# Shorter inverse square roots on VectorE, one tile for the query buffers, and nine feature places with a slot for lone weights

## The chip, the core and the metric

The kernel runs on one NeuronCore of a Trainium2 chip. The metric is the device time of one execution in microseconds (us). TensorE (PE) multiplies matrices, VectorE (DVE) and ScalarE (ACT) do elementwise work and move results out of PSUM, GpSimd (POOL) does a little elementwise work, and SyncE (SP) issues DMA transfers. Each engine runs its own instruction list strictly in order; engines wait for each other through semaphores.

## The reference

One block of a network over 2048 tokens of width 1024, with a context of 256 tokens. Both streams are normalised and modulated, projected by one matrix `w_in`, and mixed by 4 gated linear-attention heads (HGRN2) and 4 retention heads, in both directions. Output projection, residual, second norm, a feed-forward part with a convolution of width 3, and a final norm follow.

```python
hx = rmsnorm(x, norm1_g) * (1 + sc1) + sh1            # sc1, sh1 ...: silu(c) @ w_mod + b_mod
hc = rmsnorm(ctx, norm1_g) * (1 + csc1) + csh1
hq, hi, hff, hfb, hg, rq, rk, rv, rg = split(h @ w_in)   # for h = hx and h = hc, 4 heads of 128 each
f = lb + (1 - lb) * sigmoid(hff)                       # and hfb for the backward direction; k = 1 - f
# HGRN2, each direction:   S = diag(f) S + k v^T ;  o = S q      (start state from the context)
hg_o  = rmsnorm((o_f + o_b) * sigmoid(hg), hg_norm_g)
# retention, each direction: R = gamma R + k v^T ;  y = R q      (rope on q and k)
ret_o = rmsnorm(y_f + y_b, ret_norm_g) * silu(rg)
x = x + g1 * (concat(hg_o, ret_o) @ w_out)
gate, up = split((rmsnorm(x, norm2_g) * (1 + sc2) + sh2) @ w_up)
x = x + g2 * ((silu(conv3(gate)) * up) @ w_down)
return rmsnorm(x, final_g)
```

## The kernel before

Every big product is done by `mm3`: both operands are stored as pairs of f16 values (a high part and a remainder), and three matmuls (lines 102 to 104) add high by high, high by low and low by high. On top of that a product of 2 x 2 blocks is done with seven products instead of eight, so each operand exists as seven combined blocks. Seven such blocks of a group of 512 tokens are the **feature blocks**: tiles `hx` for the main stream (512 KB each), `hc` for the context. A combined block is made by a sum on VectorE (lines 455 and 501), a cast to f16 on ScalarE (450) and a subtraction that leaves the remainder on VectorE (451). For each group the tiles of temporary results that `first_blocks` uses are named in a list by `temps`: a string is one tile with both halves side by side, so that cast and subtraction are wide (128x512 in the trace); a pair of names is two narrow tiles and two instructions (128x256).

The 2048 tokens are four groups, 3 down to 0. `heads` runs over 8 heads and 4 groups. Each step weaves, instruction by instruction, the sweep of one group (`hg_sweep1`, `ret_sweep1`: decay products over levels 1 to 64, scores, state updates), the second direction of the head before (`hg_sweep2`) and the projections of the next group (`hg_proj`, `ret_proj`). A projection has the units z (gates), q and vg (values and output gate); the names `pa`, `pb`, `pc`, `pd` are its PSUM results, `ct`, `cb`, `cs`, `ta`, `tb` their copies, `w_z`, `w_q`, `w_vg` the split weights. The first head's projections use feature blocks that are made in the same steps: group 2 ahead of the loop, the context and group 1 in step 0, group 0 in step 1. They are stored to DRAM (`hxd`) and every later head loads them again (`hx<-hxd`, line 557) into a ring of `RING` = 10 places of which a group takes seven.

`norm_rows` makes the norms of a group: squares summed on ScalarE and VectorE (409, 411), `ssq` (413), the inverse root, then a scaling of each tile, half on ScalarE (419) and half on VectorE (421), and `transposed` (428, PE, `tp`). The inverse root of these calls is `rstd`, six instructions on GpSimd (lines 72 to 77). A second form, `rstd_v` (84 to 90, VectorE), is called by `head_out` for every group of every head (four columns) and by the last steps of the FFN (one column); the last of these ends the kernel.

`head_weights` loads the raw weights of the next head in 512 KB tiles: two for z, one (lone) for q, two for vg; the last head has lone v and g. All share the tag `wr` with two buffers. A raw tile is squared for its norm (750), later split into f16 pairs (q: 760; pairs: 703 and 704), and its buffer falls free with the last split.

In `hg_sweep1`, K and Q hold the two directions side by side; at each level they are multiplied by running totals `T` (925 and 930), copied for the scores (`Kl` 895, `Ql` 898), and `sc` (908) and `sf` (918) are the score matmuls. The backward queries are kept in `qf` (956), one tile per group: `qf0` to `qf3`.

The code records work in program order and a scheduler with a model of each engine's time sets each engine's instruction list before the run; the list is fixed then. So a change of tiles or of one helper can move instructions elsewhere.

## Time and profile before

| what | value |
|---|---|
| median of 3 runs | 2556.37 us (2556.28 to 2559.72) |
| the profiled execution | 2557.44 us, span 2555.7 us |
| mean granted TensorE clock | 0.99 of full speed |
| GpSimd busy | 386.9 us, 377 instructions |
| DMA moved | 402.36 MB, 157 GB/s over the span |

The profile is one execution; its span is what the trace covers, and the profiled run's own time is 1.74 us longer. An instruction row gives the start in us from the span's start, the duration, engine, line of the code, operation, output<-inputs with shapes, a count where equal rows are put together, and in brackets the engine's idle time ahead of it with the instruction that ended it. A grouped row gives the count, the sum and the mean in ns of one. A window row gives its ends, its length, and busy times with counts by engine.

### The profile page before, as it was taken

What the parts mean: (1) busy time and instruction counts of PE and PEld (TensorE: products, weight loads), DVE (VectorE), ACT (ScalarE), POOL (GpSimd) and SP (SyncE); (2) the same over time, 40 slices, a digit from 0 to 9 for tenths busy, and PEclk for the clock granted to TensorE, in tenths of its full rate; (3) what the DMA queues carried; (4) which work ended last, traced back from release to release, by engine and by line L of the source; (5) the groups of instructions that cost most, each with busy time, mean ns of one, the idle gap of its engine ahead of it and who ended that gap; (6) DMA issues with size and microseconds to landing.
All of it is one profiled execution on the core that took longest, in us unless ns stands there. A gap on an engine that the chain in (4) does not pass through costs nothing.

```text
span 2555.7 us, 56261 instructions
## 1 busy us (share of the span) xinstructions
PE 2476.7 (97%) x22763; PEld 1644.6 (64%) x22763; DVE 1892.4 (74%) x4309; ACT 1354.8 (53%) x2886; POOL 386.9 (15%) x377
## 2 busy tenths in 40 slices
PE   6899999999999999999999999999999999999998
PEld 4688989898899999985454444444444444444443
DVE  6888787878677877875658888887888887224756
ACT  7786666656545544554556565555665555211221
POOL 1100000000000000001230343434343443000000
PEclk8899999999999999999999999999999999999999
DMA  8415243334466767785320233322333338534562
GB/s 313 169 63 193 90 159 131 115 124 142 162 207 211 265 213 247 254 313 194 106 78 30 85 114 120 108 107 99 110 113 104 108 130 301 205 142 157 216 221 78
DMA packets 144788, 402.36 MB, mean 157 GB/s; under 512 B 16143, under 2 KB 16371, under 8 KB 139920
## 3 DMA queue, kind: packets, MB, share of 16 engines
q1 hardware_dynamic: 134976, 381.81, 42.7%
q10 hardware_dynamic: 9248, 16.79, 2.0%
q8 instruction: 178, 2.92, 0.5%
q14 instruction: 82, 0.67, 0.1%
q0 software_dynamic: 304, 0.17, 0.0%
HBM read 302.77 MB, written 95.94 MB: 156 GB/s over the span
## 4 chain that ended last, share of the span: by engine, by line
PE 66%; DVE 16%; issue 6%; ACT 5%; DMA 5%; POOL 1%; SPq 0%; DVEq 0%; ACTq 0%; POOLq 0%
PE pa L102 7%; PE pa L103 7%; PE pa L104 7%; PE pd L104 5%; PE pd L102 5%; PE pd L103 5%; PE pc L102 3%; PE pc L104 3%; PE pc L103 3%; PE pb L102 2%; PE pb L103 2%; PE pb L104 2%; PE opp L103 2%; PE opp L104 2%; PE opp L102 2%
## 5 line engine op out<-in xcount | busy, mean ns | idle before, releaser
L104 PE MATMUL pa<-feat,w 128*128 128x512 f16 x704 | 266.6, 379 | 1.9 <-DVE w L704 1.9
L102 PE MATMUL pa<-feat,w 128*128 128x512 f16 x704 | 263.6, 379 | 4.6 <-ACT ta L596 4.5
L103 PE MATMUL pa<-feat,w 128*128 128x512 f16 x704 | 266.8, 379 | 0.0
L103 PE MATMUL pd<-wd,actl 128*128 128x512 f16 x616 | 233.3, 379 | 0.0
L104 PE MATMUL pd<-wd,actl 128*128 128x512 f16 x616 | 233.3, 379 | 0.0
L102 PE MATMUL pd<-wd,actl 128*128 128x512 f16 x616 | 232.6, 379 | 0.0
L104 PEld LDWEIGHTS <-w 128*128 128x128 f16 x1232 | 120.5, 98 | 147.5 <-DVE w L704 2.6
L103 PEld LDWEIGHTS <-w 128*128 128x128 f16 x1232 | 120.5, 98 | 144.9 <-issue 5.3
L102 PEld LDWEIGHTS <-w 128*128 128x128 f16 x1232 | 120.4, 98 | 142.1 <-ACT w L703 1.3
L103 PEld LDWEIGHTS <-hx 128*128 128x128 f16 x1824 | 179.4, 98 | 8.3 <-issue 6.4
L102 PEld LDWEIGHTS <-hx 128*128 128x128 f16 x1824 | 179.6, 99 | 1.8 <-ACT hx L447 0.2
L104 PEld LDWEIGHTS <-hx 128*128 128x128 f16 x1824 | 179.0, 98 | 1.4 <-DVE hx L448 0.7
L1507 POOL TENSOR_TENSOR ssq<-ssq 128x1 f32<-128x1 f32 x16 | 7.0, 439 | 1111.4 <-ACT junk L1502 1111.4
L1752 ACT ACTIVATE st<-act,modT 128x512 f16<-128x512 f32 x154 | 107.3, 717 | 114.8 <-DVE act L1742 64.9
L102 PE MATMUL pa<-w_vg,hx 128*128 128x128 f16 x896 | 160.6, 220 | 3.0 <-ACT ct L596 1.4
L104 PE MATMUL pa<-w_vg,hx 128*128 128x128 f16 x896 | 160.4, 220 | 0.5 <-DVE hx L448 0.5
L1753 DVE SCALAR_TENSOR_TENSOR st<-act,modT,st 128x512 f16<-128x512 f32 x154 | 142.6, 961 | 24.5 <-ACT st L1752 23.9
L103 PE MATMUL pa<-w_vg,hx 128*128 128x128 f16 x896 | 160.7, 220 | 0.0
L102 PE MATMUL pa<-hx,w_z 128*128 128x256 f16 x512 | 140.9, 275 | 6.4 <-ACT ct L596 4.1
L104 PE MATMUL pa<-hx,w_z 128*128 128x256 f16 x512 | 140.8, 275 | 1.9 <-issue 1.9
L103 PE MATMUL pa<-hx,w_z 128*128 128x256 f16 x512 | 140.9, 275 | 0.5 <-DVE hx L451 0.4
L102 PE MATMUL pc<-feat,w 128*128 128x512 f16 x352 | 133.4, 379 | 0.8 <-ACT w L703 0.8
(545 smaller groups left out, 7219.0 us busy)
## 6 DMA issues: line engine op xcount, KB each, us to landing
hx<-hxd SPq DMA_DIRECT2D x212, 512.0 KB, 5.0
actd<-st SPq DMA_DIRECT2D x154, 256.0 KB, 2.0
actl<-actd SPq DMA_DIRECT2D x28, 1024.0 KB, 5.2
wur<-in_w_up_dram SPq DMA_DIRECT2D x44, 512.0 KB, 3.6
raw<-in_w_in_dram SPq DMA_DIRECT2D x36, 512.0 KB, 4.7
wm<-in_w_mod_dram SPq DMA_DIRECT2D x64, 256.0 KB, 4.2
hxd<-hx SPq DMA_DIRECT2D x28, 512.0 KB, 3.6
wdb<-in_w_down_dram SPq DMA_DIRECT2D x44, 256.0 KB, 4.1
```

The lines of the kernel that those rows point to most:

```text
L102: mm(ps, lhs(0), rhs(0), start=start, stop=False, skip_group_check=True)
L103: mm(ps, lhs(0), rhs(1), start=False, stop=False, skip_group_check=True)
L104: mm(ps, lhs(1), rhs(0), start=False, stop=stop, skip_group_check=True)
L1507: nc.gpsimd.tensor_tensor(ssq[:, 0:1], ssq[:, 0:1], ssq[:, 1:2], ALU.add)
L1752: nc.scalar.activation(p[:, 0], v, AF.Copy, scale=s)
L1753: nc.vector.scalar_tensor_tensor(p[:, 1], v, s, p[:, 0], ALU.mult, ALU.subtract)
```

## The change

1. `rstd_v` has 9 instructions instead of 12: the shift goes, the first guess is made in one integer multiply and add, and one polynomial with four constants takes the place of three Newton steps. It is called 48 times.
2. `norm_rows` calls `rstd_v` for the context and for groups 2, 1 and 0; only group 3 keeps the GpSimd root.
3. Q of a group is one 128 x 1024 product instead of two of 128 x 512 (16 times).
4. The four query tiles are one tile `qfs`. A pair of neighbours can then be one place for temporary blocks: in group 1 seven pairs of narrow casts and subtractions become seven wide ones.
5. `RING` goes from 10 to 9. The place is used for a new tag `wx`, one buffer, for the lone raw weights (q of heads 1 to 3, v of the last head). The shared `wr` is then for pairs (and the lone g).

VectorE has 4166 instructions instead of 4301, ScalarE 2581 instead of 2588, GpSimd 358 instead of 382. SyncE issues the same transfers in another order, and TensorE has the same instructions.

```diff
-RING = 10
+RING = 9
+RSQ = 0.7235660666409525, -0.6910196001212606, 0.7162674493934401, -0.8287177420385489
...
         ts(v, ssq, 1.0 / count, EPS, ALU.mult, ALU.add)
-        ts(t.bitcast(I32), v.bitcast(I32), 1, None, ALU.logical_shift_right)
-        ts(y.bitcast(I32), t.bitcast(I32), -1, 0x5F3759DF, ALU.mult, ALU.add)
-        for _ in range(3):
-            stt(t, y, -0.5, y, ALU.mult, ALU.mult)
-            tt(t, t, v, ALU.mult)
-            stt(y, t, 1.5, y, ALU.add, ALU.mult)
+        ts(y.bitcast(I32), v.bitcast(I32), -0.5, float(0x5F3759DF), ALU.mult, ALU.add)
+        tt(t, y, y, ALU.mult)
+        tt(t, t, v, ALU.mult)
+        ts(v, t, RSQ[0], -RSQ[0], ALU.mult, ALU.add)
+        stt(t, v, RSQ[3], v, ALU.add, ALU.mult)
+        stt(t, t, RSQ[2], v, ALU.add, ALU.mult)
+        stt(t, t, RSQ[1], v, ALU.add, ALU.mult)
+        stt(y, t, 1.0, y, ALU.add, ALU.mult)
...
+        self.qfs = mp.tile([P, NG, G], F32, name="qfs")
...
-        r = self.rstd(self.mp, ssq[:, :nt], nt, D)
+        r = self.rstd(self.mp, ssq[:, :nt], nt, D) if g == NG - 1 else self.rstd_v(ssq[:, :nt], nt, D)
...
-            def load(cols=cols, raws=raws, tags=own.get(nm, ("wr", "wr"))):
+            def load(cols=cols, raws=raws, tags=own.get(nm, ("wx",) if nm in "qv" else ("wr",) * len(cols))):
...
-        for d in range(2):
-            nc.vector.tensor_tensor(Q[:, d], qs, FG[:, 1 - d], ALU.mult)
+        nc.vector.tensor_tensor(Q, view(qs, 0, [[0, 2], [1, G]]), view(FG, G, [[-G, 2], [1, G]]), ALU.mult)
...
-                self.mp.tile([P, G], F32, tag=f"qf{slot}", bufs=1, name="qf"))
+                self.qfs[:, slot])
...
-                blocks = self.first_blocks(1, rows(1, zq), self.temps(("ou1", "ou2", ("qf1", "qf2"), "ou3")), "tu")
+                blocks = self.first_blocks(1, rows(1, zq), self.temps(("ou1", "ou2", self.qfs[:, 1:3], "ou3")), "tu")
...
-                blocks = self.first_blocks(0, rows(0, zq), self.temps(("ou2", "ou3", ("qf2", "qf3"), ("gate", "gate"))), "tu")
+                blocks = self.first_blocks(0, rows(0, zq), self.temps(("ou2", "ou3", self.qfs[:, 2:4], ("gate", "gate"))), "tu")
```

In the rows below the changed kernel's line numbers are a few higher than the old one's (925 is 930, 930 is 935, 750 is 756).

First VectorE in step 1, where group 0 is normalised while the sweep of group 2 runs (`x` are the rows to be scaled, `T_...` the running totals). Before:

```order
L413 TENSOR_TENSOR ssq<-sq_2158 128x4
L791 TENSOR_TENSOR T_1930<-T_1891 128x32
L630 TENSOR_TENSOR ct<-pc,ct 128x256
L925 TENSOR_TENSOR K<-K,T_1891 128x2x16x16
L421 TENSOR_SCALAR x_2142<-x_2142,rs_y 128x512
L421 TENSOR_SCALAR x_2144<-x_2144,rs_y 128x512
L421 TENSOR_SCALAR x_2146<-x_2146,rs_y 128x512
L421 TENSOR_SCALAR x_2148<-x_2148,rs_y 128x512
L930 TENSOR_TENSOR Q<-Q,T_1891 128x2x16x16
```

The changed kernel at the same place, from the third instruction of the root's chain:

```order
L87 TENSOR_TENSOR rs_t<-rs_y 128x4
L88 TENSOR_TENSOR rs_t<-rs_t,rs_v 128x4
L89 TENSOR_SCALAR rs_v<-rs_t 128x4
L930 TENSOR_TENSOR K<-K,T_1922 128x2x8x32
L935 TENSOR_TENSOR Q<-Q,T_1922 128x2x8x32
L90 SCALAR_TENSOR_TENSOR rs_t<-rs_v 128x4
L636 TENSOR_TENSOR ct<-pc,ct 128x256
L797 TENSOR_TENSOR T_2252<-FG 128x512
L91 SCALAR_TENSOR_TENSOR rs_t<-rs_t,rs_v 128x4
L930 TENSOR_TENSOR K<-K,T_2252 128x2x128x2
L92 SCALAR_TENSOR_TENSOR rs_t<-rs_t,rs_v 128x4
L93 SCALAR_TENSOR_TENSOR rs_y<-rs_t,rs_y 128x4
```

The scaling of x stood ahead of the 16x16 and 8x32 levels of Q; now both levels of Q stand ahead of the end of the root, and the scaling behind it.

Next SyncE while head 1 is swept and the weights of head 2 are loaded. The raw rows of both kernels read alike; before, the first of these three is head 2's lone q and the next two are its vg:

```order
L557 DMA hx<-hxd_128 128x2048
L557 DMA hx<-hxd_127 128x2048
L742 DMA raw<-in_w_in_dram 128x1024
L557 DMA hx<-hxd_146 128x2048
L557 DMA hx<-hxd_147 128x2048
L742 DMA raw<-in_w_in_dram 128x1024
L557 DMA hx<-hxd_151 128x2048
L742 DMA raw<-in_w_in_dram 128x1024
```

In the changed kernel the lone q of head 2 is the first of the three that stand together, some twenty transfers earlier, with the pair for z behind it:

```order
L748 DMA raw<-in_w_in_dram 128x1024
L563 DMA hx<-hxd_148 128x2048
L563 DMA hx<-hxd_139 128x2048
L563 DMA hx<-hxd_140 128x2048
L748 DMA raw<-in_w_in_dram 128x1024 x3
L563 DMA hx<-hxd_144 128x2048
```

The load of q no longer stands behind the reloads of the group; it is issued when head 1's split of q has run.

Last ScalarE one head on, around the split of head 2's q. Before:

```order
L760 ACTIVATE w_q<-raw,p2s 128x512 x2
L972 COPY ou<-op 128x512
L782 ACTIVATE FG<-pa,dq 128x256
L937 COPY A<-sf 64x4x64 x2
L679 ACTIVATE cs<-pa,dq 128x256
L895 COPY Kl<-K 128x512
L693 ACTIVATE qs<-pa,dq 128x256
L750 ACTIVATE w_vg,ssqw<-raw 128x1024
```

The changed kernel:

```order
L766 ACTIVATE w_q<-raw,p2s 128x512 x2
L788 ACTIVATE FG<-ct,dq 128x256
L977 COPY ou<-op 128x512
L788 ACTIVATE FG<-pa,dq 128x256
L942 COPY A<-sf 64x4x64 x2
L685 ACTIVATE cs<-pa,dq 128x256
L756 ACTIVATE w_q,ssqw<-raw 128x1024
L900 COPY Kl<-K 128x512
L699 ACTIVATE qs<-pa,dq 128x256
```

The square of head 3's q now stands behind the copy to cs, six rows after the split that frees its slot, and ahead of a copy of Kl.

## The prediction

> **What bounds the kernel now.** I read the busy times first, then the stages, then the places inside a stage where TensorE stands still, since TensorE has almost no slack elsewhere.

> ```profile
> PE 2476.7 (97%) x22763; PEld 1644.6 (64%) x22763; DVE 1892.4 (74%) x4309; ACT 1354.8 (53%) x2886; POOL 386.9 (15%) x377
> 0.00:60.00 60.00, 40.16 (x284) 25.63 (x285) 40.71 (x118) 44.85 (x80) 7.99 (x21) 0.83 0.87 333
> 60.00:205.00 145.00, 128.59 (x1940) 112.73 (x1938) 127.06 (x313) 119.53 (x283) 11.92 (x24) 0.93 0.34 127
> 205.00:705.00 500.00, 486.37 (x8408) 449.44 (x8405) 390.44 (x1065) 316.75 (x777) 0.00 (x0) 0.99 0.41 136
> 705.00:1205.00 500.00, 489.90 (x5578) 440.02 (x5579) 384.57 (x1048) 247.83 (x620) 7.57 (x28) 1.00 0.69 238
> 1205.00:2540.00 1335.00, 1325.37 (x6532) 614.10 (x6531) 940.56 (x1737) 624.40 (x1126) 359.42 (x304) 1.00 0.37 132
> 106.70:110.10 3.40, 3.40 (x18) 2.33 (x17) 0.23 (x2) 3.25 (x8) 0.00 (x0) 0.50 0.00 0
> 154.50:161.20 6.70, 6.35 (x97) 6.00 (x98) 5.81 (x13) 5.06 (x12) 0.00 (x0) 0.50 0.02 4
> 332.00:335.30 3.30, 3.30 (x18) 2.35 (x16) 1.25 (x5) 1.62 (x4) 0.00 (x0) 0.50 0.61 243
> ```

> After the page's line on engines come windows: length, then busy time of TensorE, its weight loads, VectorE, ScalarE, GpSimd, then the granted clock, DMA share and GB/s. TensorE is busy for 97% of the span, so only its gaps and the stretches at a lower clock can be won. Its idle time is 19.8 us up to 60, 16.4 from 60 to 205 (feature blocks and norms), 13.6 and 10.1 in the two sweep stages and 9.6 in the 1335 us of the output and the FFN. The last three rows are stretches at clock 0.50: what runs in them takes twice as long, so each costs half its length: 1.7, 3.35 and 1.7 us. The change touches the stages from 60 to 1205 and the very end. The profiled run took 2557.44 us (span 2555.7), 1.07 above the median of 2556.37; the sum is made against 2557.44 and taken over to the median.

> **The end of the kernel.** The last root is alone on VectorE, and the store hangs on it.

> ```profile
> 2548.85 0.15 DVE L84 TENSOR_SCALAR rs_v<-cw 128x1 f32<-128x1 f32 x1
> 2550.97 0.16 DVE L90 SCALAR_TENSOR_TENSOR rs_y<-rs_t,rs_y 128x1 f32<-128x1 f32 x1
> 2551.16 1.42 DVE L1915 SCALAR_TENSOR_TENSOR c<-c,rs_y,fgb 128x512 f32<-128x512 f32 x2
> ```

> These are the first and last of 12 dependent instructions, and the scaling that follows: 2.31 us from 2548.85 to 2551.16, or 0.1925 each. Three fewer: **-0.58 us**, on the path, nothing beside it.

> **The norms of the groups.** Four roots go from GpSimd (6 instructions each) to VectorE (9 each). First group 2 and the context, then group 1, then group 0.

> ```profile
> 64.92 0.16 DVE L413 TENSOR_TENSOR ssq<-sq 128x4 f32<-128x4 f32 x1
> 65.00 0.69 DVE L411 SCALAR_TENSOR_TENSOR junk<-gate 128x512 f16<-128x512 f32 x1
> 68.25 1.68 DVE L421 TENSOR_SCALAR x<-x,rs_y 128x512 f32<-128x512 f32 x4 [1.21 <-POOL rs_y L77]
> 75.00:100.00 25.00, 16.62 (x168) 11.47 (x166) 24.51 (x52) 23.96 (x59) 1.00 (x1) 0.80 0.61 230
> ```

> A bracket is the idle time ahead of the instruction and what ended it. A small instruction with independent work behind it occupies VectorE for 0.08 us (64.92 to 65.00), a dependent one for 0.19. From 75 to 100 VectorE is busy for 24.51 of 25 us, so what two roots add there or just ahead counts in full: 18 instructions, at 0.08 to 0.1925, are 1.4 to 3.5 us; taken at 0.10, near the interleaved price since context work is at hand, 1.8. The idle 1.21 goes. Net **+0.6** (from -1.2, if the additions fall in other gaps, to +3.5, if the idle time comes back).

> ```profile
> 99.00 3.12 POOL L72 TENSOR_SCALAR rs_v<-ssq 128x4 f32<-128x4 f32 x1 [28.55 <-DVE ssq L413]
> 104.12 0.20 POOL L77 TENSOR_TENSOR rs_y<-rs_y,rs_t 128x4 f32<-128x4 f32 x1
> 104.35 1.67 DVE L421 TENSOR_SCALAR x<-x,rs_y 128x512 f32<-128x512 f32 x4 [2.30 <-POOL rs_y L77]
> 104.99 0.58 PE L428 MATMUL tp<-ident,x 128*128 128x128 f32 x3 [1.95 <-DVE x L421]
> 144.95 0.19 POOL L72 TENSOR_SCALAR rs_v<-ssq 128x4 f32<-128x4 f32 x1 [40.63 <-DVE ssq L413]
> 147.95 1.68 DVE L421 TENSOR_SCALAR x<-x,rs_y 128x512 f32<-128x512 f32 x4 [2.02 <-POOL rs_y L77]
> 152.50 0.68 DVE L930 TENSOR_TENSOR Q<-Q,T 128x512 f32<-128x512 f32 x1
> 153.33 0.69 PE L918 MATMUL sf<-Q,K 128*64 128x64 f32 x16 [2.20 <-DVE Q L930]
> ```

> In group 1 the GpSimd chain lasts 5.32 us (99.00 to 104.32); nine instructions on VectorE take 1.73 alone, but 3.2 us of other VectorE work stand in the same stretch. The scaling can start at 102.9 to 103.8 instead of 104.35, so of TensorE's 1.95 us some 0.6 to 1.5 go; I take 1.0. The half-clock stretch that begins at 106.7 is worth 1.7; I take 0.5 of it, since much of the gap remains. **-1.5** (0 to -3.65).

> In group 0 VectorE idles 2.02 us for the root and then scales four tiles (1.68) before the levels of Q on which TensorE waits 2.20 us. Now that Q stands ahead of the scaling and independent levels lie between the root's instructions (nine at 0.10, 0.9 us), Q comes up to 2.02 + 1.68 - 0.9 = 2.8 us earlier, more than the gap: -2.2, and of the 3.35 of the half-clock stretch behind it 0.8. **-3.0** (0 to -5.55). What is late next are the scaled tiles: their transposes have about the cover they had.

> **Wide blocks, one Q.**

> ```profile
> L451 DVE TENSOR_TENSOR hx<-ftmp,hx 128x512 f16<-128x512 f32 x28 | 18.8, 684 | 1.0 <-ACT hx L450 0.9
> L451 DVE TENSOR_TENSOR hx<-ftmp,hx 128x256 f16<-128x256 f32 x28 | 11.0, 417 | 0.9 <-ACT hx L450 0.9
> L872 DVE TENSOR_TENSOR Q<-qs,FG 128x512 f32<-128x512 f32 x32 | 20.7, 684 | 3.4 <-ACT qs L693 3.4
> ```

> Fourteen half-width subtractions become seven wide ones: 7 x (2 x 417 - 684) = 1.05 us of VectorE, and as many casts go from ScalarE. Both have idle time behind 105 us: **-0.3** (0 to -1.0). Sixteen Q products lose one instruction start each, at 0.08 that is 1.3 us of VectorE, beside TensorE's sweeps; it is counted with the next term.

> **Roots in the sweeps.**

> ```profile
> L84 DVE TENSOR_SCALAR rs_v<-ossq 128x4 f32<-128x4 f32 x32 | 5.3, 166 | 20.7 <-ACT qf L996 20.6
> ```

> 32 calls lose 3 instructions: 7.7 us of VectorE at 0.08, 18.5 at 0.1925. VectorE idles for 109 and 115 us in these two stages while TensorE idles for 23.7, so TensorE's own work covers most of it; if that cover were gone, all 18.5 would count. **-2** (0 to -5), nearer to nothing because the chain itself waits 20.6 us for ScalarE. The 16 one-column roots of the FFN lie beside full TensorE: 0, but for the last.

> **The lone query weights.**

> ```profile
> 224.47 1.33 ACT L760 ACTIVATE w_q<-raw,p2s 128x512 f16<-128x512 f32 x2
> 254.69 1.06 ACT L750 ACTIVATE w_z<-raw 128x1024 f16<-128x1024 f32 x1 [4.25 <-DMA raw<-in_w_in_dram]
> 324.45 0.33 SPq L742 DMA_DIRECT2D raw<-in_w_in_dram  x1
> 330.17 1.06 ACT L750 ACTIVATE w_q<-raw 128x1024 f16<-128x1024 f32 x1 [2.62 <-DMA raw<-in_w_in_dram]
> 327.89 0.22 PE L102 MATMUL pa<-w_vg,hx 128*128 128x128 f16 x1 [0.33 <-DVE cb L630]
> 331.63 0.27 PE L102 MATMUL pa<-hx,w_z 128*128 128x256 f16 x1 [2.24 <-ACT ct L596]
> 347.95 1.32 ACT L760 ACTIVATE w_q<-raw,p2s 128x512 f16<-128x512 f32 x2
> 350.90 0.47 ACT L679 ACTIVATE cs<-pa,dq 128x256 f32<-128x256 f32 x1
> 352.53 0.86 ACT L895 COPY Kl<-K 128x512 f32<-128x512 f32 x1 [1.15 <-DVE K L870]
> 479.39 0.22 PE L102 MATMUL pa<-w_vg,hx 128*128 128x128 f16 x1 [0.32 <-DVE cb L630]
> 481.69 0.27 PE L102 MATMUL pa<-hx,w_z 128*128 128x256 f16 x1 [0.80 <-ACT ct L596]
> ```

> Head 2's query weights are asked for at 324.45, when a shared slot falls free, and ScalarE stands for them until 330.17 with the eviction behind it that TensorE needs. With their own slot they are asked for behind head 1's split (224.47) and squared soon after, and the row is gone from this place. Counted: 2.24, the half clock from 332 (1.7), the same gap of 0.80 at head 3, and 0.33 and 0.32 in the small gaps ahead of these: **-5.4** (-2.5, if another raw weight takes the place, to -6.5). But the new slot is freed by the split of the head before, and the next square now stands six rows behind that split. At head 3 the split ends at 349.3, the row ahead of the square (the copy to cs) at 351.4, and a load of this kind took 5.7 us above (324.45 to 330.17): a new ScalarE wait of 2 to 3.6 us, with the copy of Kl behind it that had 1.15 us of slack. **+1.0** (0 to +2.5). Head 2's square stands eight rows behind that split, in a stretch where ScalarE waited 4.25 us for another raw (254.69) and no gap of TensorE followed: 0.

> **Nine places instead of ten.**

> ```profile
> hx<-hxd SPq DMA_DIRECT2D x212, 512.0 KB, 5.0
> ```

> The page's row on reloads of feature blocks: 212 of them, 5.0 us to land. They lie in the 1000 us of the two sweep stages, one per 4.7 us. Seven places belong to the group in work, so three loads ran ahead and now two: by this estimate 9.4 us of cover against 5.0. Where loads bunch, some come late: **+1** (0 to +4).

> **Sum:** -0.6 + 0.6 - 1.5 - 3.0 - 0.3 - 2.0 - 5.4 + 1.0 + 1.0 = -10.2 us: 2547.2 as a profiled run, **2546.2 us** as a median.

> [...] The granted clock stood at 0.50 from 332, right behind a gap of 2.24 us. [...]

> **The rivals.**
> *The gaps close and the half-clock stretches stay.* The sum counted 1.7 + 0.5 + 0.8 = 3.0 for the clock: 2549.2. For it: these gaps are short. Against it: all three stretches start within 2 us of one.
> *The waits only move.* Raw weights still arrive one behind the other and VectorE is full from 75 to 100. If the norms bring nothing (+4.5 against the sum) and head 3's new wait is 2.5 and stalls TensorE as the old one did (+1.5 and the clock, 1.7), the sum is -2.5: 2553.9, within 0.2% (5.1 us, about what a measurement of this kernel can tell from no change).
> *More.* If all the clock comes back (+3.75) and the sweeps give their 5, it is 2546.2 - 6.75 = 2539.5.
> *Slower: the ring of nine.* A group's first reload now waits for one more release. Once loads in a bunch land later than 9.4 us, each of some 30 groups (212 / 7) stalls TensorE. To end above 2561.5 this must cost 15.3 us, 0.5 per group; with 0.6 it is 18, and the time 2563. For it: loads already stand behind each other in one queue. Against it: 5.0 us to land.

> **How the numbers follow.** The sum as it stands 0.40 (own range 2542 to 2551), half clock stays 0.15, more 0.15, waits move 0.21, slower 0.09. The first three are faster: 0.70; same 0.21; slower 0.09. The range 2539 to 2556 takes in all but the slower case and the far end of "more".

> **What will show it.** The last root with 9 instructions, 1.73 us. No POOL wait ahead of the scalings of groups 1 and 0; TensorE's gap of 2.20 on Q gone. No raw load ahead of w_q near 330, no gap of 2 us there, clock 1.0 from 332 to 335; a new ScalarE wait of 2 to 3.6 us on a raw near 351. TensorE's idle time from 60 to 205 below 13 us. Reload waits no larger than before. I am wrong if the half clock stays without a gap, if reloads stall the first projection of a group, or if VectorE's work ahead of 100 us delays the context features by more than the norms save.

## The result, and the profile after

The changed kernel takes 0.9929 of the time before (95% interval 0.9918 to 0.9939), some 18 us less; in a second session 0.9923 (0.9911 to 0.9935). The median is 2540.28 us (6 runs, 2536.66 to 2542.58). The kernel before, run beside it, had 2559.27 (6 runs, 2556.28 to 2561.57). The forecast was 2546.2, range 2539 to 2556: the direction held and the median lies in the range, but the gain is 18 us and not 10. The forecast set out from 2556.37; the ratio on that time gives 2538.2, just under the range, so it is in part luck of the session that the range held.

The page's line on engines of the changed kernel, whose profiled run took 2539.82 us (span 2538.0), and then windows as before:

```profile
PE 2470.5 (97%) x22763; PEld 1640.2 (65%) x22763; DVE 1877.6 (74%) x4174; ACT 1354.5 (53%) x2879; POOL 375.9 (15%) x353
```

```profile
60.00:205.00 145.00, 129.90 (x2051) 115.22 (x2048) 136.25 (x346) 123.78 (x283) 0.00 (x0) 0.96 0.36 133
205.00:705.00 500.00, 493.01 (x8474) 457.31 (x8472) 386.88 (x1031) 319.21 (x788) 0.00 (x0) 1.00 0.41 134
705.00:1205.00 500.00, 492.46 (x5479) 435.02 (x5477) 378.12 (x977) 251.43 (x621) 11.78 (x42) 1.00 0.71 245
325.00:335.00 10.00, 10.00 (x176) 9.07 (x175) 7.13 (x27) 7.16 (x19) 0.00 (x0) 1.00 0.22 84
90.50:100.70 10.20, 5.85 (x38) 4.51 (x37) 10.20 (x28) 8.58 (x27) 0.00 (x0) 0.50 0.51 206
384.00:387.40 3.40, 3.40 (x64) 3.20 (x64) 2.32 (x10) 2.29 (x9) 0.00 (x0) 0.50 0.34 104
```

TensorE does the same instructions. Its idle time in the first sweep stage fell from 13.6 to 7.0 us and in the second from 10.1 to 7.5; from 60 to 205 us it fell only from 16.4 to 15.1. The clock is 1.00 from 325 to 335. Between 60 and 1250 us three stretches at half clock are left: 10.24 us from 90.46, and 3.41 us each from 384.00 and 1025.71. Summed over the trace from 60 to 1250 us, the gaps between TensorE's instructions were 40.1 us and are 29.6, and the time lost to half clock (half of each such stretch: in the one from 331.95 before, the 128x256 matmuls start 0.21 us apart, from 336.37 on 0.11) was 13.7 us and is 8.5. These 15.6 us, 0.6 at the end and 1.4 ahead of 50 us are 17.6 of the 17.7 by which the spans differ.

Where the time came from, by instructions that occur equally often in both kernels (start in the changed kernel less start before, the median over all instructions of a stretch of 25 us; the column on the left is the time before):

| at | difference | since the row above |
|---|---|---|
| 50 | -1.4 | -1.4 |
| 75 to 100 | -0.5 | +0.9: context features |
| 275 to 325 | -7.5 | -7.0: norms of groups 1 and 0, blocks |
| 325 to 350 | -11.7 | -4.1: the gap at 330 |
| 425 to 475 | -10.1 | +1.6 |
| 550 to 575 | -10.6 | -0.6 |
| 600 to 625 | -12.5 | -1.9 |
| 700 to 725 | -16.4 | -3.9: the stall at 671 |
| 1200 | -18.2 | -1.9 |
| 2150 to 2500 | -17.1 | +1.1 |
| end | -17.7 | -0.6 |

At the end the root now lasts from 2531.77 to 2533.50, 1.73 us:

```profile
2531.77 0.15 DVE L85 TENSOR_SCALAR rs_v<-cw 128x1 f32<-128x1 f32 x1
2533.50 1.41 DVE L1920 SCALAR_TENSOR_TENSOR c<-c,rs_y,fgb 128x512 f32<-128x512 f32 x2
```

The gap at 330 is gone; the new wait of ScalarE that the prediction named is there, one head on, and the third row is a gap of TensorE further on that was not foreseen, with the half clock from 384.00 behind it:

```profile
340.80 1.06 ACT L756 ACTIVATE w_q<-raw 128x1024 f16<-128x1024 f32 x1 [1.84 <-DMA raw<-in_w_in_dram]
343.44 0.72 ACT L900 COPY Kl<-K 128x512 f32<-128x512 f32 x1 [0.39 <-DVE K L930]
383.19 0.22 PE L105 MATMUL pc<-w_vg,hx 128*128 128x128 f16 x1 [1.98 <-ACT qs L699]
```

### The profile page after: what moved, and what is told of

It reads as the page before. It is cut to its first block, busy times and chain, and to the rows that moved or that the text cites. A ratio compares the mean times of both kernels' runs of the same rounds, so it can differ in the third digit from the quotient of the medians.

```text
span 2538.0 us, 56102 instructions
## 1 busy us (share of the span) xinstructions
PE 2470.5 (97%) x22763; PEld 1640.2 (65%) x22763; DVE 1877.6 (74%) x4174; ACT 1354.5 (53%) x2879; POOL 375.9 (15%) x353
## 4 chain that ended last, share of the span: by engine, by line
PE 71%; DVE 13%; DMA 6%; ACT 6%; issue 3%; POOL 1%; SPq 0%; DVEq 0%; ACTq 0%; POOLq 0%
PE pa L105 8%; PE pa L106 8%; PE pa L107 8%; PE pd L107 5%; PE pd L106 5%; PE pd L105 5%; PE pc L105 4%; PE pc L106 4%; PE pc L107 4%; PE pb L105 2%; PE pb L106 2%; PE pb L107 2%; PE opp L105 2%; PE opp L106 2%; PE opp L107 2%
## 5 line engine op out<-in xcount | busy, mean ns | idle before, releaser
L106 PEld LDWEIGHTS <-hx 128*128 128x128 f16 x1824 | 179.3, 98 | 10.2 <-issue 8.4
## 6 DMA issues: line engine op xcount, KB each, us to landing
hx<-hxd SPq DMA_DIRECT2D x212, 512.0 KB, 4.9
wur<-in_w_up_dram SPq DMA_DIRECT2D x44, 512.0 KB, 3.6
raw<-in_w_in_dram SPq DMA_DIRECT2D x36, 512.0 KB, 5.3
hxd<-hx SPq DMA_DIRECT2D x28, 512.0 KB, 3.2
```

What stands on the lines that cost most here:

```text
L106: mm(ps, lhs(0), rhs(1), start=False, stop=False, skip_group_check=True)
```

## The experiments

Ratios are to the kernel before in the same session, with 95% intervals. Four runs do one part alone, three undo one part of the changed kernel, the rest test a place.

**The short root alone.** The kernel before with the new `rstd_v` (the first hunk of the change).

> The kernel before with the root of 9 instructions in all 48 calls and nothing else of the change. Theory 1 (the shorter chain itself frees ScalarE and TensorE in the sweeps): the stall of 2.2 us on KTt near 671 and the half clock behind it go (-3.6), 2 to 4 us come from other places of the sweeps, 0.58 at the end: 6 to 8 us faster than before. Theory 2 (the sweeps gained because the whole instruction order changed, not because of the chain): only the 0.58 at the end and at most 1.5 elsewhere, 0.6 to 2 us faster. In both the gap of 2.24 us at 330 and the norms' waits stay as before.

0.9971 (0.9959 to 0.9983), 7.4 us faster, the size that theory 1 had. One place is the stall near 671. Before, TensorE waited there for a copy that stood in ScalarE's list behind the square of the next head's z:

```profile
670.83 1.06 ACT L750 ACTIVATE w_z<-raw 128x1024 f16<-128x1024 f32 x1 [3.49 <-DMA raw<-in_w_in_dram]
672.35 0.59 ACT L948 COPY KTt<-kp 128x512 f32<-128x512 f32 x1
672.99 1.83 PE L952 MATMUL uf<-V,KTt 128*128 128x128 f32 x8 [2.23 <-ACT KTt L948]
```

The raw weights come late because their slot is freed by the last splits of w_vg on VectorE; the load is issued at 666.25, right behind the split of 665.47. These splits stand among the 12 steps of a root. The rows are the first step, that split, the last step, the scaling that uses the root, and TensorE's transposes of its result (`otp`) and of K (`kp`), which is the last work ahead of the stall:

```profile
659.98 0.17 DVE L84 TENSOR_SCALAR rs_v<-ossq 128x4 f32<-128x4 f32 x1 [0.46 <-ACT qf L996]
665.47 0.75 DVE L704 SCALAR_TENSOR_TENSOR w_vg<-raw,p2s,w_vg 128x512 f16<-128x512 f32 x1
667.79 0.16 DVE L90 SCALAR_TENSOR_TENSOR rs_y<-rs_t,rs_y 128x4 f32<-128x4 f32 x1
667.99 0.69 DVE L1018 TENSOR_TENSOR ou<-ou,rs_y 128x512 f32<-128x512 f32 x1
669.28 0.60 PE L1003 MATMUL otp<-ident,ou 128*128 128x128 f32 x4
669.72 1.04 PE L947 MATMUL kp<-ident,K 128*128 128x128 f32 x8
```

The root with the splits between its steps takes 8 us. In the changed kernel it takes 5.2, the load is issued at 653.45, ScalarE waits 1.51 us and TensorE 0.29:

```profile
652.67 0.75 DVE L710 SCALAR_TENSOR_TENSOR w_vg<-raw,p2s,w_vg 128x512 f16<-128x512 f32 x1
653.34 0.68 DVE L1023 TENSOR_TENSOR ou<-ou,rs_y 128x512 f32<-128x512 f32 x1
655.28 0.60 PE L1008 MATMUL otp<-ident,ou 128*128 128x128 f32 x4
655.72 1.04 PE L952 MATMUL kp<-ident,K 128*128 128x128 f32 x8
658.07 1.06 ACT L756 ACTIVATE w_z<-raw 128x1024 f16<-128x1024 f32 x1 [1.51 <-DMA raw<-in_w_in_dram]
659.75 1.16 PE L957 MATMUL uf<-V,KTt 128*128 128x128 f32 x8 [0.29 <-ACT KTt L953]
```

The shorter root did not bring the weights sooner. Counted from an earlier split of w_vg (ends at 659.51 and 646.71) the load is issued 6.74 us later in both kernels, ScalarE's square starts 4.58 and 4.62 us behind the load, and TensorE has started 10074 and 10073 matmuls when it is issued. What moved is the work behind the root. The scaling starts 1.74 us behind the load before, and 0.11 us ahead of it now; so `otp` and `kp` stand earlier in TensorE's list, and 33 matmuls of the projections stand between `kp` and the wait where there were none. TensorE falls idle 6.00 us behind the load instead of 4.51. On ScalarE the copy of `otp` now stands ahead of the square and takes up part of its wait.

With the short root alone the stall is gone too, in the same way. By common instructions 2.6 us of its gain lie here, and some 6 us between 900 and 1200, where TensorE's gaps of 1.0 to 1.8 us at 1014, 1042, 1070 and 1126 are gone or 0.8 at most. A new wait of 2.06 us on KTt at 548 and the half clock behind a gap of 2.13 at 478 take some 5 back.

**The long root in the changed kernel.**

> The changed kernel with the old root of 12 instructions in all calls (sweeps, norms and the end). Theory 1 (chain length matters in the sweeps): 6 to 8 us slower than the changed kernel, with a stall near 660 again. Theory 2 (order, not chain): 1 to 3 us slower, of which 0.58 at the end and up to 1 in the norms.

0.9950 (0.9937 to 0.9962), some 5 us slower than the changed kernel, between the two theories. The stall of TensorE on KTt is back, at 656, with 2.11 us, and no half clock behind it. In all 14 profiles it goes with the root: 1.55 to 2.93 us in the six kernels with 12 instructions, 0.41 or less in the eight profiles with 9. The order goes with it: TensorE falls idle 4.51 us behind the load in all of the six, and runs on until 5.84 to 6.10 us behind it in the eight. That much is shown; that the scheduler sets the transposes earlier because the root's result is ready earlier in its model is argued. In the norms the length made no difference: up to 200 us the two kernels keep step within 0.9 us.

**The slot alone.** The kernel before, with

```diff
-RING = 10
+RING = 9
...
+            def load(cols=cols, raws=raws, tags=own.get(nm, ("wx",) if nm in "qv" else ("wr",) * len(cols))):
```

> The kernel before with nine feature places and the own slot for lone raw weights, nothing else. Theory 1 (the gap at 330 and its half clock go, the new wait of ScalarE one head on costs TensorE little): 4 us gained at 330, 0 to 2 given back from 350 to 425, about 1 gained at 480: 3 to 5 us faster. Theory 2 (nine places cost what the slot gains, since reloads come later): within 1 us of before, with larger waits for hx. The half clock at 332 is a test of its own: if it stays at 0.50 without a gap ahead of it, the gap was not its cause.

0.9967 (0.9955 to 0.9980), 8.4 us faster, more than either theory. The gap at 330 is gone with its half clock (-4.1 by common instructions), as theory 1 said, but 3.4 us came between 100 and 200 us, where no lone weight is loaded: TensorE's wait of 2.20 us on Q was gone, with the norms on GpSimd. The next run was made for that.

**Nine places alone.** `RING = 9` and nothing else.

> The kernel before with nine feature places instead of ten and nothing else: lone weights still share. It does no work less, but the order of the instructions moves. If a place less costs cover, it is 1 to 4 us slower than before, with new waits on hx. If the slot's run gained from 100 to 205 (3.4 us there, where the slot has no load) by the new order that nine places bring, this run is 2 to 4 us faster than before and the wait of 2.20 us at 151 is gone, while the gap of 2.2 us near 330 stays.

0.9980 (0.9969 to 0.9991), 5 us faster, by a change that only takes a buffer away. The scheduler made another order. The wait of 2.20 us on Q at 151 is gone, and the same stretch shows how. VectorE before (prediction) waited 2.02 us for the root; here more work stands in front of it, a second eviction among it, GpSimd's root takes 2.4 us instead of 3.0, and the wait is 0.66:

```profile
146.00 0.42 DVE L630 TENSOR_TENSOR ct<-pc,ct 128x256 f32<-128x256 f32 x1
147.08 1.67 DVE L421 TENSOR_SCALAR x<-x,rs_y 128x512 f32<-128x512 f32 x4 [0.66 <-POOL rs_y L77]
149.27 0.68 DVE L930 TENSOR_TENSOR Q<-Q,T 128x512 f32<-128x512 f32 x1
```

The gap near 330 stays, shorter (1.54 us) and without the half clock, and the one near 478 has grown from 0.80 to 2.56. By the ratios about 3 of the 8.4 us belong to the slot and 5 to the order that came with nine places; but each ratio is known to some 3 us either way, so this split is an estimate. ScalarE's waits for reloads of hx are 3.2 and 3.7 us (at 979 and 1121), where the kernel before has 2.5, 2.3 and 3.2 (734, 983, 1126) and the changed kernel one of 1.1 (1013).

**The shared slots back in the changed kernel** (ten places, no `wx`).

> The changed kernel with ten feature places and all raw weights in the two shared slots. Theory 1 (the slot's gain is the gap at 330): the gap of about 2 us and the half clock come back there, 3 to 5 us slower than the changed kernel. Theory 2 (nine places cost as much as the slot gains): the same time within 1 us.

0.9935 (0.9922 to 0.9947), 1.5 us slower than the changed kernel by the ratios, within their intervals. By common instructions it is 3.0 to 4.3 us behind from 600 to 1100 us; a gap of 1.47 us on the raw weights stands at 323 and one of 1.25 at 471, without half clock behind them. A gap of 2.00 us on KTt at 539, where no lone weight is loaded, costs as much. In exchange the gap of 1.98 us at 381 is gone.

**The norms alone, with the long root.**

```diff
-        r = self.rstd(self.mp, ssq[:, :nt], nt, D)
+        r = self.rstd(self.mp, ssq[:, :nt], nt, D) if g == NG - 1 else self.rstd_v(ssq[:, :nt], nt, D)
```

> The kernel before with the norms of the context and of groups 2, 1 and 0 on VectorE, with the old root of 12 instructions, nothing else. Theory 1 (the norms' own waits are what the stage from 100 to 205 gained): the stage from 100 to 205 is 4 to 7 us shorter, the waits of 1.95 and 2.20 us and the half clock behind them go, and the stage before 100 is up to 2 us longer: 3 to 6 us faster. Theory 2 (that stage gained through the new order, since the run with the slot alone lost the wait of 2.20 us too): 0 to 3 us faster, and a wait of about 2 us stands elsewhere in the stage.

0.9981 (0.9971 to 0.9990), 4.9 us. By common instructions some 7 us were gained from 60 to 205, with both waits gone (theory 1), and some 5.5 given back behind a gap of 1.96 us on Kl at 214 and one of 2.30 on ct at 473, this one with half clock.

**The norms back on GpSimd in the changed kernel.**

> The changed kernel with the norms back on GpSimd. Theory 1: 3 to 6 us slower than the changed kernel, with waits of about 2 us on rs_y of GpSimd and half clock in the stage from 100 to 160. Theory 2: within 3 us of it.

0.9936 (0.9919 to 0.9953), 1.8 us slower by the ratios, 3.7 by the trace. TensorE's gap ahead of the transposes of group 1 is back (2.38 us at 101), the one on Q is not.

**The rest: wide blocks and one Q product**, in the kernel before.

> The kernel before with the rest of the change: one tile for the queries with wide blocks in group 1, and one Q product. My sum said 0.3 for the blocks and next to nothing for Q: within 1.5 us of before if only the work counts. If the order of instructions counts as much as the work, anything from 4 us faster to 2 slower, with gaps of 1 to 2 us at other places than before.

0.9996 (0.9984 to 1.0007): no gain that can be measured, as the sum had it, though gaps moved (1.04 instead of 2.20 us at 148, a new one of 2.09 at 173).

**Eight places and two slots for lone weights.**

> The changed kernel with eight feature places and two buffers for lone raw weights. If reloads had cover to spare (my estimate: 4.7 us of cover per place, 5.0 us to land, so one place ahead is the border) the wait of 1.84 us on a raw near 341 goes and nothing else changes: 0 to 2 us faster than the changed kernel. If a place less costs cover, TensorE or ScalarE wait for hx in many groups: 5 to 20 us slower. Small waits on hx in the last heads alone would give 1 to 4 us slower.

0.9929 (0.9912 to 0.9946), the time of the changed kernel. The wait at 341 is gone; TensorE's gap of 1.98 us at 382 is still there, so that wait does not make it. One reload is late, with 1.36 us of ScalarE at 1070 and a gap of TensorE of 2.04 there: nine places had cover to spare nearly everywhere.

**The norms divided.** In the changed kernel the context and group 2 go back to GpSimd, groups 1 and 0 stay on VectorE.

```diff
-        r = self.rstd(self.mp, ssq[:, :nt], nt, D) if g == NG - 1 else self.rstd_v(ssq[:, :nt], nt, D)
+        r = self.rstd(self.mp, ssq[:, :nt], nt, D) if g in (None, 2, NG - 1) else self.rstd_v(ssq[:, :nt], nt, D)
```

> The changed kernel with the norms of the context and group 2 on GpSimd and those of groups 1 and 0 on VectorE. If the instructions of two roots on a full VectorE cost what the comparison shows from 75 to 100 (0.9 us) and more behind it, TensorE's wait of 3.8 us near 90 falls to about 2.7 and the half clock behind it (10.2 us long) is halved: 1 to 4 us faster than the changed kernel. If GpSimd's chain is late there too: the same or 1 us slower.

0.9918 (0.9898 to 0.9938). Since that interval overlaps the changed kernel's, both ran again in one session:

> The version with the norms of the context and group 2 on GpSimd and those of groups 1 and 0 on VectorE, once more with more rounds. If its gain of 2.8 us over the changed kernel was real: 2 to 4 us faster than it in the same session. If it was the luck of one session: within 1 us.

> The changed kernel once more, for a second profile of the same instruction lists and beside the next run. Gaps of TensorE at the same places with the same lengths within 0.2 us; the half-clock stretches behind gaps of about 2 us may come or go, since a stretch follows when the idle time falls into one interval of 3.41 us. 16 to 20 us faster than before.

The divided version 0.9902 (0.9887 to 0.9916), 2532.48 us (2527.88 to 2534.87, 4 runs); the changed kernel 0.9923, 2537.47 (2535.87 to 2538.79, 5 runs). The ranges do not touch, though the intervals of the ratios do: 5 us faster by the medians, and the fastest version here. By common instructions 3.6 us are gained up to 105 us in the second pair of profiles. TensorE's longest waits from 84 to 102 us, first of the changed kernel (three rows), then of the divided one (three rows):

```profile
88.41 0.22 PE L106 MATMUL pa<-hc,w_z 128*128 128x128 f16 x1 [1.52 <-DVE hc L455]
94.30 0.27 PE L106 MATMUL pa<-hc,w_z 128*128 128x128 f16 x1 [3.80 <-DVE hc L455]
97.31 0.37 PE L105 MATMUL pa<-hx,w_z 128*128 128x256 f16 x1 [0.55 <-ACT ct L602]
```

```profile
85.77 0.27 PE L106 MATMUL pa<-hc,w_z 128*128 128x128 f16 x1 [1.63 <-DVE hc L455]
91.59 0.27 PE L105 MATMUL pb<-hc,w_z 128*128 128x128 f16 x1 [2.71 <-DVE ct L636]
93.39 0.37 PE L106 MATMUL pa<-hx,w_z 128*128 128x256 f16 x1 [0.36 <-DVE hx L455]
```

The longest wait of this stretch is 3.8 to 4.1 us in each kernel whose roots of the context and group 2 run on VectorE, and about 2.7 in each where they run on GpSimd: VectorE is full here (10.20 of 10.20 us from 90.5 in the changed kernel), and GpSimd's root cost less than VectorE's instructions do. The second profile of the changed kernel has most of its gaps at the same places (1.51, 3.80, 1.43, 1.98), one of 1.81 at 579 that the first had not, and 0.54 at 1023 where the first had 1.44.

## Why the prediction was right, and where its sum was off

- **The end**, -0.58: 1.73 us instead of 2.31, as worked out.
- **Group 2 and the context**, +0.6: +0.9, and the divided version shows that this was the wrong trade: the price was in TensorE's wait for context features.
- **Group 1**, -1.5: the gap of 1.95 us went whole, with its half clock. The step that failed is the start of the scaling: it does not begin at 102.9 to 103.8 but at 105.30, since the root's nine instructions were spread over other work (100.13 to 105.26). The transposes have no gap ahead because TensorE now has other work in front of them:

```profile
100.13 0.16 DVE L85 TENSOR_SCALAR rs_v<-ssq 128x4 f32<-128x4 f32 x1
105.10 0.16 DVE L93 SCALAR_TENSOR_TENSOR rs_y<-rs_t,rs_y 128x4 f32<-128x4 f32 x1
105.30 1.67 DVE L425 TENSOR_SCALAR x<-x,rs_y 128x512 f32<-128x512 f32 x4
106.91 1.36 PE L432 MATMUL tp<-ident,x 128*128 128x128 f32 x11
```

  The gap is there in every kernel whose group 1 root is on GpSimd (1.95 to 2.38) and in none where it is on VectorE, so the move does it, but through the order and not through an earlier root.
- **Group 0**, -3.0: the gap of 2.20 and its half clock went, 5.5 us by the rows of the prediction. But nine places alone remove it with the root on GpSimd. Taking away the cause I gave (the wait for GpSimd) removes the gap; another order does so too.
- Together the stage from 100 to 205 gave 7.0 where the terms and the blocks said 4.8: too little of the half clock was counted. One sign failed: TensorE's idle time from 60 to 205 was to be below 13 us and is 15.1, since from 60 to 100 it rose from 8.4 to 9.9 with the wait for context features, and from 160 to 205 from 2.4 to 3.8.
- **The lone weights**, -5.4: -4.1 at 330 and -0.6 near 480. The new wait, +1.0, came with 1.84 us (2 to 3.6 forecast) and cost TensorE nothing there. The 1.6 us given back up to 425 stand at another place, the gap of 1.98 us at 381 and the half clock from 384.00: the copy of qs behind a block of small ScalarE instructions that prepare the retention heads.
- **Nine places**, +1: 0. The estimate of one reload per 4.7 us made its cover look thinner than it is; with eight places one wait of 1.36 us is listed and the time is the same.
- **The sweeps**, -2: this is the term that was mis-sized. About -7.7 came there (1.9 near 600, 3.9 near 671, 1.9 from 725 to 1200). The rule I took, that TensorE's work covers VectorE's, fails where the scaling behind a root, and with it TensorE's transposes, stand so late in the order that TensorE has nothing else in front of its next wait: near 671 it then stands for a load that, counted by TensorE's own work, comes no later than in the changed kernel. The trace before had 3.41 us at half clock behind this stall, from 673.28, which stands in no term of the sum. A row of the waits pointed at the place; it stands first, and behind it that of the changed kernel (us in total, times, longest):

```profile
ACT w_z L750 <- DMA raw<-in_w_in_dram: 26.8, 11, 4.3
```

```profile
ACT w_z L756 <- DMA raw<-in_w_in_dram: 13.4, 12, 2.1
```

  With the short root alone the sum is 18.8, and 21.4 in the changed kernel with the long one. What lies behind the 1.9 from 725 to 1200 was not traced. Since the stretch near 600 had a gap in the second profile again, that 1.9 is not a settled gain.
- **In no term** stand the -1.4 ahead of 50 us, whose cause is open, and the +1.1 behind 1200, where a stretch at half clock from 2104.32 is in this profile of the changed kernel and not in its second.
- **The rivals.** Where the gap went, the half clock went (330, 103, 151, 671), against the first rival, short as these gaps were (1.95 to 2.24 us). "More" (2539.5, chance 0.15) came nearest. In the rival of the ring 15.3 is worked out with the term of 1.0 still in the sum, and 2563 without it; without it, the 15.3 is 16.3. The parts alone add up to 21.7 us (7.4, 8.4, 4.9, 1.0) against some 18 for all, while undoing one costs 1.5 to 5, each known to some 3 us either way: each part also brings a new order that is some microseconds better or worse by itself, as nine places alone show. How much of each part's gain is order and how much is work is settled only for the places named here.

## What to carry to other kernels

With a scheduler that fixes the order, a change that does no work less can be worth as much as one that does (5 us for a buffer fewer), so test each part alone and undone, and judge by the gap that comes and goes with it. A chain of small instructions can cost by what stands behind its result: at each wait of the full engine, follow the wait back to its reader, the load and the slot, and then see whether these moved or the work that the full engine has in front of them. Before you move work from a slow engine to a fast one (GpSimd's root lasted 3.0 and 5.32 us in groups 0 and 1 before, VectorE's of nine instructions 1.73 alone at the end), look at whether the fast one is full at that place; here VectorE was (10.20 of 10.20 us from 90.5), and two of four norms were better left on GpSimd.

## What the runs showed of the hardware

```profile
329.07 0.27 PE L105 MATMUL pa<-hx,w_z 128*128 128x256 f16 x1 [2.09 <-ACT ct L599]
478.00 0.37 PE L105 MATMUL pa<-hx,w_z 128*128 128x256 f16 x1 [2.13 <-ACT ct L599]
```

```profile
327.70:331.10 3.40, 2.03 (x19) 1.81 (x19) 1.05 (x6) 3.27 (x8) 0.00 (x0) 1.00 1.00 398
477.90:481.30 3.40, 3.30 (x16) 2.31 (x16) 1.58 (x4) 2.09 (x6) 0.00 (x0) 0.50 0.77 308
```

The gap of 2.09 us ended at 329.07, across the border at 327.7, and the clock stayed at 1.00; of the one of 2.13 that ended at 478.00, 1.99 lay ahead of the border at 477.86, within one interval, and the clock fell to 0.50. In these runs, then, some 2 us of idle time within one interval of 3.41 were enough. Runs of one kernel differ by a few us (2536.66 to 2542.58 for the changed kernel), and its two profiles show where: the first, 3.0 us longer, has stretches at half clock from 1025.71 and 2104.32 that the second lacks, and the gaps just ahead of them were longer in it (1.44 us against 0.54 near 1023, 3.15 against 2.05 near 2100). Whether the place of a gap on the grid alone can make such a difference is not shown.
